# Remainders of the sparse attention's keys in one half of the partitions, and their logits pass over 64 rows

## The chip, the cores and the metric

The kernel runs on one core of one Trainium2 chip. The metric is the device time of one execution in microseconds (us): the median of three runs of the kernel before is 1380.08 us (1379.23 to 1384.18). A core has a matrix engine (PE, with its weight loads shown as PEld), a vector engine (DVE), an engine for activations (ACT), a general engine (POOL) and one that issues transfers (SP). They work through queues of their own and wait for each other by semaphores.

## The reference

One layer of a decoder trunk, 1024 tokens wide 1024, all in f32. A combined projection feeds three groups: a gated linear recurrence (4 heads, HGRN2), a sparse attention (4 heads of 64) and a cross-attention to 256 memory tokens. A projection back and a gated feed-forward follow. The change concerns the sparse attention alone:

```python
def dsa_mix(q, k, v, iq, ik, iw, q_gain, k_gain):
    ...
    q = rmsnorm(q, q_gain).astype(f32)
    k = rmsnorm(k, k_gain).astype(f32)
    ...
        score = jnp.where(visible[None], score, -jnp.inf)
        _, idx = lax.top_k(score, topk)
        ...
        logits = jnp.einsum('bqhd,bqkhd->bhqk', qb, kg) * (SA_DH ** -0.5)
        logits = jnp.where(valid[:, None], logits, -jnp.inf)
        p = jax.nn.softmax(logits, axis=-1)
        return jnp.einsum('bhqk,bqkhd->bqhd', p, vg)
```

The kernel does not gather keys: it computes the logits of all keys up to the end of the query's block and adds a mask of the kept ones.

## The kernel before, in words

**Precision.** The matmuls of f32 operands run in fp32r. For them an operand is written as a head (`hi`, an ACT copy into fp32r) and a remainder (`lo`, the operand minus its head), and a product is built from hi x hi, hi x lo and lo x hi.

**Operands of the sparse attention.** A head has 64 dimensions, half of the 128 partitions. Heads come in pairs: pair m holds head h = 2m + j in the partitions `ROWS[j]`, 0 to 63 or 64 to 127. For queries, `stack` (lines 245 to 255) writes the head of the query into `ROWS[j]` of a tile `qst[h][hf]` and its remainder into the other half, so that one tile of 128 partitions holds both (`hf` is the half of the 1024 tokens). For keys, lines 807 to 819 fill two tiles per head and half: `kst[h][0]` has the key's head in both halves of the partitions (two ACT copies, L818), `kst[h][1]` the key's remainder in both halves (two subtractions, L819: DVE writes the head's own half, POOL the other one).

**Logits.** `sa_logits` runs over blocks of 128 queries from the last (b = 7) to the first, and over 4 heads. A block sees 128 (b + 1) keys, taken in chunks of up to 512 columns, each chunk with a PSUM bank of its own (tag `lg`). A chunk is two matmuls that add up (L838): the query tile is the stationary operand, 128 rows by 128 columns; the moving operand is `kst[h][0]` and then `kst[h][1]`. The first gives (hi + lo of q) x hi of k, the second (hi + lo of q) x lo of k. There are 48 chunks. DVE then adds the mask and takes the maximum (L840).

**Order.** The stages of an item (logits; exponential on ACT and scaling on POOL, L849 and L855; transposes on PE, L864; the product with the values, L883, whose output is 64 partitions wide) run as a pipeline of four, and between its steps stand `fillers`: the last head of the recurrence (L518 to L612) and first parts of the output projection (L186). A scheduler that follows a model of the time sets the order on each engine. The names: `sap` is the preparation of the sparse attention, `sat` the attention, `hg` the recurrence, `wo` the output projection; `sap_h` are the tiles of `qst` and `kst`.

L271, which is named later, transposes eight rows of indexer weights with eight matmuls of 8 rows at partition 64; L117 and L118 split an operand into head and remainder; L144 to L151 are the small steps of an inverse root on DVE.

Of the kernel before, what the change touches and what calls it, by code (L numbers as in the profile page):

```python
# [9 lines left out]
F32 = mybir.dt.float32  # L10
# [5 lines left out]
AF = mybir.ActivationFunctionType  # L16
# [26 lines left out]
def hybrid_block(ctx, tc, xT, memT, wch, wikw, wv, wkm, wvm, woa, wob, wfi, wfo,  # L43
                 vec, cst, lvl, out):
    nc = tc.nc
    V, S, G, T = nc.vector, nc.scalar, nc.gpsimd, nc.tensor
# [13 lines left out]
    def nm(p):  # L60
        cnt[0] += 1
        return f"{ph[0]}_{p}{cnt[0]}"
# [4 lines left out]
    def bank(tag):  # L67

        return pp.tile([128, 512], F32, tag=tag, name=nm(tag))

    def xt(i, shape, dt=F32):
        return xp.tile(shape, dt, tag=f"x{i}", name=nm(f"x{i}_"))
# [4 lines left out]
    def ht(p, k, hf):  # L77
        return hp.tile([128, 512], F32R, tag=f"h{p}{k}{hf}", name=nm("h"))

    def hs(hf):  # L80
        return slice(hf * 512, hf * 512 + 512)

    def bs(b):
        return slice(b * 128, b * 128 + 128)
# [160 lines left out]
    def stack(st, ps, hf, rs, gain=None):  # L245

        o = slice(64 - rs.start, 128 - rs.start)
        if gain is None:
            S.activation(st[rs, hf], ps[rs], AF.Copy)
            V.tensor_sub(st[o, hf], ps[rs], st[rs, hf].bitcast(F32))  # L250
        else:
            g = vs[rs, gain:gain + 1]
            S.activation(st[rs, hf], ps[rs], AF.Copy, scale=g)
            V.scalar_tensor_tensor(st[o, hf], ps[rs], g, st[rs, hf].bitcast(F32),
                                   op0=ALU.mult, op1=ALU.subtract)

    ROWS = (slice(0, 64), slice(64, 128))
# [53 lines left out]
    for k in range(8):  # L311
        src = mT[k // 4][:, k % 4, :]
# [13 lines left out]
    for m in range(2):  # L326
# [15 lines left out]
        r = bank("sm")[:, :256]  # L342
        token_rows(r, rk, 2)
        V.scalar_tensor_tensor(kr, kr, vs[:, V_MK:V_MK + 1], r, op0=ALU.mult, op1=ALU.mult)
        for j in range(2):
            rs = slice(64 * j, 64 * j + 64)
# [4 lines left out]
    for g in range(2):  # L351
        w = load_page(wvm[g], 4, 256)
        for tt in range(2):
            i = 0
            for pw, p in PASSES:
                for k in range(4):
                    T.matmul(acc[tt][:, :256], mn[p][g][:, k, bs(tt)], w(pw, k),
                             start=g == 0 and i == 0, stop=g == 1 and i == 11)
# [10 lines left out]
    for t2 in range(4):  # L369
# [3 lines left out]
        for b in range(2, 8):  # L373
            for j in range(2):
                h = 2 * t2 + j
                for c0 in range(0, 128 * (b + 1), 512):
                    c1 = min(128 * (b + 1), c0 + 512)
                    lg = bank(("lg", "rc")[j])
                    for p in range(2):
                        T.matmul(lg[:, :c1 - c0], iqs[t2 % 2][j][:, b // 4, bs(b % 4)], ik[p][:, c0:c1],  # L380
                                 start=p == 0, stop=p == 1)
# [25 lines left out]
    def q_scale():  # L407

        wide = lambda t: t.unsqueeze(2).to_broadcast([128, 8, 2])
        for m in range(2):  # L410
            V.tensor_mul(qrs[:, m], qsq[:, m], wide(rn2))
        flat = qrs.rearrange("p a b c -> p (a b c)")
        narrow_rstd(flat, flat, 64, 32)
        for m in range(2):
            V.scalar_tensor_tensor(qrs[:, m], qrs[:, m], 0.125, wide(rn), op0=ALU.mult,
                                   op1=ALU.mult)
# [379 lines left out]
    qst = [[None, None] for _ in range(4)]  # L796
# [9 lines left out]
    kst = [[[None, None], [None, None]] for _ in range(4)]  # L806
    for hf in range(2):
        for m in range(2):
            for j in range(2):
                h = 2 * m + j  # L810
                if m == 0:
                    qst[h][hf] = ht(0, h, hf)
                    stack(qst[h][hf].unsqueeze(1), sqr[0][:, hs(hf)], 0, ROWS[j], V_SAQ)
                for p in range(2):
                    kst[h][p][hf] = ht(1 - p, h + 4 * p, hf)
                src = kr[m][ROWS[j], hs(hf)]
                for o, e in ((ROWS[j], V), (ROWS[1 - j], G)):
                    S.activation(kst[h][0][hf][o], src, AF.Copy)  # L818
                    e.tensor_sub(kst[h][1][hf][o], src, kst[h][0][hf][ROWS[j]].bitcast(F32))  # L819
    q_scale()  # L820

    ph[0] = "sat"
# [3 lines left out]
    def sa_logits(t):  # L826
        b, h = t["b"], t["h"]
        nk = 128 * (b + 1)
        m, j = h // 2, h % 2
        i = t["i"]  # L830
        mask = sc[b] if b >= 2 else tri[:, 128 * (1 - b):256]
        P = t["P"] = xt((0, 1, 12)[i % 3], [128, 1024])
        mx = t["mx"] = np_.tile([128, 3], F32, tag="mz", name=nm("mz"), bufs=5)
        for c in range(0, (nk + 511) // 512):
            c0, c1 = 512 * c, min(nk, 512 * c + 512)
            lg = bank("lg")
            for p in range(2):
                T.matmul(lg[:, :c1 - c0], qst[h][b // 4][:, bs(b % 4)],  # L838
                         kst[h][p][c][:, :c1 - c0], start=p == 0, stop=p == 1)
            V.tensor_tensor_reduce(P[:, c0:c1], lg[:, :c1 - c0], mask[:, c0:c1], 1.0,  # L840
                                   -3.0e38, ALU.add, ALU.max, mx[:, c:c + 1])
        rq = t["rq"] = qrs[:, m, b, j:j + 1]
        if nk > 512:
            V.tensor_max(mx[:, 0:1], mx[:, 0:1], mx[:, 1:2])
        V.scalar_tensor_tensor(mx[:, 0:1], mx[:, 0:1], -1.0, rq, op0=ALU.mult, op1=ALU.mult)
# [51 lines left out]
    def sparse_attention():  # L897
        items = [dict(b=b, h=h, i=4 * n + h) for n, b in enumerate(range(7, -1, -1))
                 for h in range(4)]
        return pipeline(items, (sa_logits, lambda t: (sa_exp(t), sa_scale(t)), sa_turn, sa_out))  # L900
# [275 lines left out]
    for n, j in enumerate([2 * i for i in range(NP)] + [2 * i + 1 for i in range(NP)]):  # L1176
        if n < 12:
            wo_[j] = halves(xt(PAGES[n], [128, 1024]))
        else:
            i, hf = divmod(n - 12, 2)  # L1180
# [88 lines left out]
    def four(slot, m, hf):  # L1269

        t = []

        def add(store):
            def begin():
                if not t:
                    t.extend(again(slot, m, hf) + again(slot + 1, m + 2, hf))
                return done

            def done(i, ps):
                V.tensor_add(t[i], t[i], ps)  # L1280
                if store:
                    nc.sync.dma_start(out[bs(m + i), hs(hf)], t[i])
            return begin
        return add
# [3 lines left out]
    c = four(0, 0, 0)  # L1288
# [85 lines left out]
```

## Time and profile before

| | |
|---|---|
| median of 3 runs | 1380.08 us (1379.23 to 1384.18) |
| the profiled execution | 1380.01 us |
| its span, first to last instruction | 1378.2 us, mean granted clock of TensorE 0.973 |
| PE busy | 1299.7 us (94%), 8072 matmul records |
| DVE busy | 1051.9 us (76%) |
| ACT busy | 691.2 us (50%) |
| POOL busy | 476.4 us (35%) |
| the chain that ended last | PE 68%, DVE 20%, ACT 7% of the span |

The busy shares are averages over a long program. The preparation of the sparse attention, the attention and the feed-forward behind it have different limits, so the view of a stretch tells more than these shares. The end of a matmul's record is modelled; the distance from one start to the next tells what it costs.

### The profile page before, as it was taken

To read this page: it belongs to the slowest core of one execution; us is meant where nothing else is said; L and a number is where in the kernel's file an instruction comes from. 1 tells how busy PE (TensorE), PEld (TensorE's weight loads), DVE (VectorE), ACT (ScalarE), POOL (GpSimd) and SP (SyncE) were. 2 spreads that over 40 slices of the span, in tenths; PEclk is the share of its full clock that TensorE was granted. 3 is DMA by queue.
4 is the path that set the end of the run, shared out by engine and by line. 5 is a ranking of instruction groups with operands and counts; after the bars stand their busy time and mean duration, and the time that the engine had idled before them with its cause. 6 is when DMAs were issued, how large, how long until landed. Compare 5 with 4: busy or idle time off the path is not lost.

```text
span 1378.2 us, 21967 instructions
## 1 busy us (share of the span) xinstructions
PE 1299.7 (94%) x8072; PEld 1067.1 (77%) x8072; DVE 1051.9 (76%) x2027; ACT 691.2 (50%) x1369; POOL 476.4 (35%) x395
## 2 busy tenths in 40 slices
PE   7989999989999995999997999999999998999998
PEld 4767797769887874876886888888888887878887
DVE  8696998895486789775679778777787766696764
ACT  7555879968823252756454333333333334334442
POOL 2311134364375642424005233332332210484520
PEclk9999999979999996899999999999999999999999
DMA  6110010000101101013331332222222219754241
GB/s 238 64 45 16 17 50 29 32 32 33 46 17 47 36 17 47 2 62 129 122 109 62 115 115 100 99 86 106 100 103 104 92 55 352 242 192 144 84 146 62
DMA packets 53245, 122.19 MB, mean 89 GB/s; under 512 B 6033, under 2 KB 6161, under 8 KB 53137
## 3 DMA queue, kind: packets, MB, share of 16 engines
q1 hardware_dynamic: 52848, 120.58, 25.2%
q8 instruction: 63, 1.03, 0.3%
q14 instruction: 46, 0.37, 0.1%
q10 hardware_dynamic: 288, 0.22, 0.1%
HBM read 92.19 MB, written 28.57 MB: 88 GB/s over the span
## 4 chain that ended last, share of the span: by engine, by line
PE 68%; DVE 20%; ACT 7%; issue 3%; DMA 1%; POOL 1%; DVEq 0%; SPq 0%; ACTq 0%; POOLq 0%
PE ff_lg L1103 17%; PE ff_rc L1103 12%; PE hg_mm L186 4%; PE fo_mm L1266 4%; PE fo_sm L1266 4%; DVE idx_x L646 4%; PE wo_mm L1062 3%; PE fo_rc L1266 3%; PE fo_lg L1266 3%; PE wo_sm L1062 2%; PE sap_mm L186 2%; PE idx_mm L186 2%; ACT idx_x L643 1%; DVE idx_x L388 1%; PE sat_sm L864 1%
## 5 line engine op out<-in xcount | busy, mean ns | idle before, releaser
L117 ACT ACTIVATE ff_whi<-ff_x 128x512 fp32r<-128x512 f32 x112 | 70.0, 629 | 125.3 <-PE ff_rc L1103 69.1
L643 ACT ACTIVATE idx_x<-idx_x,packs 128x896 int8<-128x896 f32 (+3 forms) x128 | 105.6, 825 | 29.8 <-DVE packs L662 22.2
L1103 PE MATMUL ff_lg<-wo_h,ff_whi 128*128 128x512 f32 x396 | 104.2, 389 | 0.0
L186 PE MATMUL hg_mm<-xn_h,hg_whi 128*128 128x512 f32 x384 | 97.3, 399 | 0.0
L1103 PE MATMUL ff_rc<-wo_h,ff_whi 128*128 128x512 f32 x308 | 90.8, 395 | 0.0
L1103 PE MATMUL ff_lg<-wo_x,ff_whi 128*128 128x512 f32 x308 | 83.8, 400 | 5.6 <-ACT ff_tmp L1110 4.8
L118 DVE TENSOR_TENSOR ff_wlo<-ff_x,ff_whi 128x512 fp32r<-128x512 f32 x112 | 82.6, 745 | 7.1 <-ACT ff_whi L117 4.0
L1103 PEld LDWEIGHTS ff_lg<-wo_h,ff_whi 128*128 128x128 f32 x396 | 74.5, 188 | 15.4
L186 PEld LDWEIGHTS hg_mm<-xn_h,hg_whi 128*128 128x128 f32 x384 | 71.6, 191 | 15.0 <-issue 0.9
L118 POOL TENSOR_TENSOR hg_wlo<-hg_wst,hg_whi 128x512 fp32r<-128x512 f32 x32 | 42.9, 1357 | 112.6 <-ACT hg_whi L117 81.7
L1103 PEld LDWEIGHTS ff_lg<-wo_x,ff_whi 128*128 128x128 f32 x308 | 56.8, 189 | 24.2 <-ACT ff_whi L117 7.7
L646 DVE TENSOR_SCALAR_CACHE_REDUCE idx_x<-idx_x,packs 128x1024 int8<-128x1024 f32 x64 | 68.8, 1075 | 1.0
L1103 PEld LDWEIGHTS ff_rc<-wo_h,ff_whi 128*128 128x128 f32 x308 | 58.8, 191 | 12.4
L1103 PE MATMUL ff_rc<-wo_x,ff_whi 128*128 128x512 f32 x220 | 64.4, 390 | 0.1
L528 POOL TENSOR_TENSOR hg_x<-hg_x,hg_x 128x256 f32<-128x256 f32 x56 | 48.1, 876 | 34.5 <-PE hg_rc L518 23.4
L1103 PE MATMUL ff_lg<-wo_h,ff_wlo 128*128 128x512 f32 x198 | 55.6, 389 | 0.0
L388 DVE SCALAR_TENSOR_TENSOR idx_x<-idx_tmp,packs,idx_x 128x512 f32<-128x512 f32 (+2 forms) x70 | 46.1, 709 | 12.3 <-ACT idx_tmp L383 11.9
L118 DVE TENSOR_TENSOR fo_wlo<-fo_tmp,fo_whi 128x512 fp32r<-128x512 f32 x33 | 32.9, 996 | 27.3 <-ACT fo_whi L117 27.3
L186 PE MATMUL hg_mm<-xn_h,hg_wlo 128*128 128x512 f32 x192 | 50.9, 397 | 0.0
L1103 PEld LDWEIGHTS ff_rc<-wo_x,ff_whi 128*128 128x128 f32 x220 | 41.2, 188 | 9.1 <-ACT ff_whi L117 0.6
L1103 PE MATMUL ff_rc<-wo_h,ff_wlo 128*128 128x512 f32 x154 | 45.6, 389 | 0.0
L1041 POOL TENSOR_TENSOR ff_x<-ff_wst,ff_wst 128x512 f32<-128x512 f32 x7 | 14.0, 2003 | 91.0 <-PE wo_sm L1062 74.7
(485 smaller groups left out, 3681.3 us busy)
## 6 DMA issues: line engine op xcount, KB each, us to landing
gd<-ff_m SPq DMA_DIRECT2D x77, 256.0 KB, 2.0
fo_x<-gd SPq DMA_DIRECT2D x77, 256.0 KB, 4.1
ff_x<-wfi SPq DMA_DIRECT2D x16, 512.0 KB, 3.3
ff_wst<-wfi SPq DMA_DIRECT2D x14, 512.0 KB, 3.2
ff_m<-wfi SPq DMA_DIRECT2D x14, 512.0 KB, 3.2
hg_wst<-wch SPq DMA_DIRECT2D x12, 512.0 KB, 3.3
fo_x<-wfo SPq DMA_DIRECT2D x24, 256.0 KB, 5.2
fo_h<-wfo SPq DMA_DIRECT2D x20, 256.0 KB, 4.4
```

The source lines that it names most:

```text
L117: S.activation(hi, src, AF.Copy)
L118: (eng or V).tensor_sub(lo, src, hi.bitcast(F32))
L186: T.matmul(ps[:M, :], w(pw, k), h[p][k][hf], start=i == 0, stop=i == len(order) - 1)
L388: V.scalar_tensor_tensor(sc[b][:, c0:c1], rl[:, :c1 - c0], iww[:, b, h:h + 1], sc[b][:, c0:c1], op0=ALU.mult, op1=ALU.add)
L528: G.tensor_mul(Kv[:, :, 0, :], Kv[:, :, 0, :], fr.to_broadcast([128, n, w]))
L643: S.activation(waste[S][:, :nk], sc[b], AF.Sign, bias=fl[:, j:j + 1], accum_out=ct[:, j:j + 1])
L646: eng.tensor_scalar(waste[eng][:, :nk], sc[b], fl[:, j:j + 1], None, op0=ALU.is_ge, op1=ALU.add, accum_out=ct[:, j:j + 1])
L864: T.transpose(tb[:, bs(kb - g0)], P[:, bs(kb)], ident)
L1041: G.tensor_sub(s3, a11, a21)
L1062: mm = T.matmul(ps, lhs, rhs, start=i == 0, stop=i == len(steps) - 1)
L1103: mm = T.matmul(ps, w[pw][:, bs(k)], HB[u][k][p], start=first and i == 0, stop=i == 11, skip_group_check=True)
L1266: T.matmul(banks[m], w[i][pw][:, bs(m)], b[i][p], start=first and i == 0 and n == 0, stop=i == NP - 1 and n == 2, skip_group_check=True)
```

## The change

POOL's subtraction is gone: the key's remainder is written only into the head's own half of the partitions, by DVE as before. ACT still copies the head into both halves. In the logits the first matmul of a chunk is as before; the second takes only the 64 rows `ROWS[j]` of both operands. There the query tile holds its head, so the second product is now hi of q x lo of k, and the product of the two remainders is left out.

```diff
--- before.py
+++ after.py
@@ -814,9 +814,10 @@
                 for p in range(2):
                     kst[h][p][hf] = ht(1 - p, h + 4 * p, hf)
                 src = kr[m][ROWS[j], hs(hf)]
-                for o, e in ((ROWS[j], V), (ROWS[1 - j], G)):
-                    S.activation(kst[h][0][hf][o], src, AF.Copy)
-                    e.tensor_sub(kst[h][1][hf][o], src, kst[h][0][hf][ROWS[j]].bitcast(F32))
+                o = ROWS[j]
+                for r in (o, ROWS[1 - j]):
+                    S.activation(kst[h][0][hf][r], src, AF.Copy)
+                V.tensor_sub(kst[h][1][hf][o], src, kst[h][0][hf][o].bitcast(F32))
     q_scale()
 
     ph[0] = "sat"
@@ -834,9 +835,9 @@
         for c in range(0, (nk + 511) // 512):
             c0, c1 = 512 * c, min(nk, 512 * c + 512)
             lg = bank("lg")
-            for p in range(2):
-                T.matmul(lg[:, :c1 - c0], qst[h][b // 4][:, bs(b % 4)],
-                         kst[h][p][c][:, :c1 - c0], start=p == 0, stop=p == 1)
+            for p, rs in ((0, slice(0, 128)), (1, ROWS[j])):
+                T.matmul(lg[:, :c1 - c0], qst[h][b // 4][rs, bs(b % 4)],
+                         kst[h][p][c][rs, :c1 - c0], start=p == 0, stop=p == 1)
             V.tensor_tensor_reduce(P[:, c0:c1], lg[:, :c1 - c0], mask[:, c0:c1], 1.0,
                                    -3.0e38, ALU.add, ALU.max, mx[:, c:c + 1])
         rq = t["rq"] = qrs[:, m, b, j:j + 1]
```

On POOL, between the recurrence's steps (L528) of its head 2 and those of its head 3, stand the eight subtractions of the keys:

```order
 L528 TENSOR_TENSOR hg_x_568_3372<-hg_x_568_3372,hg_x_569_3373 128x8x32 x2
 L528 TENSOR_TENSOR hg_x_568_3372<-hg_x_568_3372,hg_x_569_3373 128x4x64 x2
-L819 TENSOR_TENSOR sap_h_5513<-sap_m_667_4665,sap_h_5512 64x512
-L819 TENSOR_TENSOR sap_h_5522<-sap_m_667_4665,sap_h_5521 64x512
-L819 TENSOR_TENSOR sap_h_5528<-sap_m_668_4666,sap_h_5527 64x512
-L819 TENSOR_TENSOR sap_h_5534<-sap_m_668_4666,sap_h_5533 64x512
-L819 TENSOR_TENSOR sap_h_5543<-sap_m_667_4665,sap_h_5542 64x512
-L819 TENSOR_TENSOR sap_h_5552<-sap_m_667_4665,sap_h_5551 64x512
-L819 TENSOR_TENSOR sap_h_5558<-sap_m_668_4666,sap_h_5557 64x512
-L819 TENSOR_TENSOR sap_h_5564<-sap_m_668_4666,sap_h_5563 64x512
 L528 TENSOR_TENSOR hg_x_642_4459<-hg_x_642_4459,hg_x_643_4460 128x256 x2
 L528 TENSOR_TENSOR hg_x_642_4459<-hg_x_642_4459,hg_x_643_4460 128x128x2 x2
```

Nothing else moves on POOL; the rows around the gap follow each other directly. On PE no instruction is added, removed or moved. One place in the attention, before, between a product with the values (L883) and the recurrence (L594); `sap_h` are the key tile and the query tile of two chunks, of 512 and 256 keys:

```order
L883 MATMUL sat_mm_6114<-sat_x_814_6050,sap_x_552_3146 64x128
L838 MATMUL sat_lg_6163<-sap_h_5521,sap_h_5548 128x512
L838 MATMUL sat_lg_6163<-sap_h_5522,sap_h_5548 128x512
L838 MATMUL sat_lg_6167<-sap_h_5551,sap_h_5548 128x256
L838 MATMUL sat_lg_6167<-sap_h_5552,sap_h_5548 128x256
L594 MATMUL hg_rc_6251<-hg_x_602_3847,hg_x_666_4648 128x128
```

The same place with the change, where lines behind 819 have a number higher by one:

```order
L884 MATMUL sat_mm_6106<-sat_x_814_6042,sap_x_552_3146 64x128
L839 MATMUL sat_lg_6155<-sap_h_5520,sap_h_5543 128x512
L839 MATMUL sat_lg_6155<-sap_h_5521,sap_h_5543 128x512
L839 MATMUL sat_lg_6159<-sap_h_5546,sap_h_5543 128x256
L839 MATMUL sat_lg_6159<-sap_h_5547,sap_h_5543 128x256
L594 MATMUL hg_rc_6243<-hg_x_602_3847,hg_x_666_4648 128x128
```

The order is the same; the second and the fourth of the L839 rows now use 64 of the array's 128 rows.

## Rows read from the trace of the kernel before

**Rows 1.** Busy time by stretch: PE, PEld, DVE, ACT, POOL, clock, DMA.
```profile
502.00:534.00 32.00, 21.70 (x110) 18.62 (x108) 30.86 (x74) 19.78 (x33) 12.42 (x8) 0.79 0.15 50
...
553.90:634.00 80.10, 79.75 (x636) 64.59 (x636) 58.09 (x213) 51.91 (x115) 26.84 (x34) 0.97 0.08 28
```

**Rows 2.** Timeline, PE: start, us, operation, idle before.
```profile
522.02 2.05 PE L172 MATMUL sap_sm<-packs,sap_tmp 128*128 128x128 f32 x8 [8.58 <-DVE sap_tmp L169]
```

**Rows 3.** Timeline, DVE, from 502 to 518 us.
```profile
503.56 1.66 DVE L819 TENSOR_TENSOR sap_h<-sap_m,sap_h 64x512 fp32r<-64x512 f32 x1
...
510.53 0.68 DVE L819 TENSOR_TENSOR sap_h<-sap_m,sap_h 64x512 fp32r<-64x512 f32 x1
...
511.14 1.25 DVE L149 SCALAR_TENSOR_TENSOR sap_abx<-sap_abx 128x8 f32<-128x8 f32 x1
...
512.42 0.17 DVE L150 TENSOR_TENSOR sap_abx<-sap_abx 128x8 f32<-128x8 f32 x1
...
516.14 0.65 DVE L150 TENSOR_TENSOR sap_abx<-sap_abx 128x8 f32<-128x8 f32 x1
```

**Rows 4.** Timeline, POOL, from 495 to 535 us.
```profile
502.37 3.98 POOL L819 TENSOR_TENSOR sap_h<-sap_m,sap_h 64x512 fp32r<-64x512 f32 x2 [12.29 <-PE sap_mm L186]
...
510.57 6.19 POOL L819 TENSOR_TENSOR sap_h<-sap_m,sap_h 64x512 fp32r<-64x512 f32 x4 [4.23 <-ACT sap_h L818]
...
526.34 2.62 POOL L819 TENSOR_TENSOR sap_h<-sap_m,sap_h 64x512 fp32r<-64x512 f32 x2 [9.57 <-ACT sap_h L818]
```

**Rows 5.** Timeline, DVE, at 526 us.
```profile
526.49 1.15 DVE L151 SCALAR_TENSOR_TENSOR hg_abx<-hg_abx 128x8 f32<-128x8 f32 x1
```

**Rows 6.** Timeline, ACT, and one operation of DVE, 509 to 525 us.
```profile
509.86 2.58 ACT L818 ACTIVATE sap_h<-sap_m 64x512 fp32r<-64x512 f32 x4 [4.21 <-DVE sap_m L752]
...
515.56 0.52 ACT L117 ACTIVATE wo_whi<-wo_wst 128x384 fp32r<-128x384 f32 x1
...
518.80 0.54 DVE L118 TENSOR_TENSOR wo_wlo<-wo_wst,wo_whi 128x384 fp32r<-128x384 f32 x1
...
524.78 0.68 ACT L253 ACTIVATE sap_h<-sap_mm,packs 64x512 fp32r<-64x512 f32 x1 [3.61 <-DVE sap_h L254]
```

**Rows 7.** Matmuls of L838 by stretch: PE, PEld, clock, DMA.
```profile
534.00:553.90 19.90, 2.04 (x4) 1.16 (x4) 0.61 0.01 3
553.90:634.00 80.10, 20.10 (x80) 12.78 (x80) 0.97 0.08 28
```

**Rows 8.** Chain that ended last, 553 to 580 us: start, us, work.
```profile
559.71 0.81 PE sat_lg L838 x4
560.52 0.44 PE sat_sm L864 x4
...
562.21 0.59 PE sat_sm L864 x4
...
563.82 1.01 PE sat_lg L838 x4
```

**Rows 9.** Timeline, PE, around L271, and eight passes at 511 us.
```profile
51.89 0.84 PE L186 MATMUL idx_mm<-xn_h,xn_wlo 128*72 128x512 f32 x3
52.66 1.05 PE L271 MATMUL idx_sm<-packs,idx_tmp 8*128 8x8 f32 x8
53.65 0.45 PE L186 MATMUL idx_mm<-xn_h,xn_wlo 128*72 128x512 f32 x1
53.93 0.64 PE L332 MATMUL mkv_mm<-mkv_x,mkv_whi 128*128 128x256 f32 x4
...
511.46 1.98 PE L186 MATMUL sap_mm<-xn_h,sap_wlo 128*128 128x512 f32 x8
```

**Rows 10.** Chain that ended last, at 536 and at 596 us.
```profile
536.44 1.71 PE sat_lg L838 x4
...
596.45 0.68 DVE wo_m L920
...
600.88 0.90 PE sat_lg L838 x4
```

## The prediction

> **What bounds the kernel now.** I read the busy time by stretch first, then the chain of work that ended last, then the timeline of single engines where the diff acts. The change touches two stretches, and they have different limits.
>
> From 502 to 534 us the keys and queries of the sparse attention are split into head and remainder. There DVE is busy 30.86 of 32.00 us and PE only 21.70 [rows 1]; PE stands still for 8.58 us until DVE has written a tile (L169) at 522 [rows 2]. What DVE does is therefore the time of this stretch. From 553.9 to 634 us, the sparse attention itself, PE is busy 79.75 of 80.10 us [rows 1] and the chain runs from one PE piece to the next. So in the first stretch microseconds are won on DVE, in the second they are lost on PE, and the diff does one of each.
>
> **First part: eight subtractions leave POOL.** They are L819's second halves, 64x512 each; DVE keeps its eight, ACT its sixteen copies (L818). The trace shows no wait for one of POOL's remainders, so its 12.4 us of POOL time [rows 1] are worth nothing as such. What counts is what DVE does while POOL runs them. At 503.56 DVE's own L819 takes 1.66 us; the same operation at 510.53, begun just before POOL's next group, takes 0.68 [rows 3]. POOL was inside L819 from 502.37 to 506.35 and from 510.57 to 516.76 [rows 4]. Long DVE operations there go from 0.68 to 1.65 or so three times (503.56, and alike at 505.24 and 512.62), which is 0.98 + 0.97 + 0.99 = 2.94. Tiny ones of 0.17 (as at 512.42) become 1.25 and 0.65, and between these 1.11 at 514.32 [rows 3]: 1.08 + 0.94 + 0.48 = 2.50. A last one, at 526.49, takes 1.15 [rows 5] under POOL's last pair [rows 4]: 0.98. In all 6.4 us of DVE's time appear only while POOL subtracts, and I expect all of it to go.
>
> How much reaches PE? ACT could take over as the limit. Its run of splits starts at 509.86, behind L752 on DVE [rows 6], thus after the first two long stalls, and comes 1.95 us earlier; ACT itself gets no faster. DVE's L118 at 518.80 needs the ACT copy of 515.56, which ends at 516.08 [rows 6], afterwards at 516.08 - 1.95 = 514.13. DVE can therefore come to it at about 514.2, 4.6 us earlier, not 2.94 + 2.50 = 5.4. Of the last 0.98 I count 0.9, because the DVE operation behind it (L840) reads PE's first logits and may have to wait for them. Together 5.5 us, between 0 (if the long DVE operations have another reason) and 6.4.
>
> **Second part: 48 remainder passes over 64 rows.** Each block of up to 512 keys has two matmuls of L838. Their moving columns stay the same, and so does the time that they stream; half the rows idle. Both instructions remain. What is new is that the array goes from 128 rows to 64 and back. The order on PE is the same, so the switches can be counted in it. In the PE-bound stretch stand 80 matmuls of L838 [rows 7], 40 remainders. Each is one switch in. Behind 13 comes the next block's full pass, behind 12 a transpose (L864, one L571), behind 5 another full matmul (L186, L578, L594); that is one switch out each. Behind the other 10 comes a half-width matmul (L883 and its like), before which the array changes its shape already. New switches: 40 + 30 = 70.
>
> Their price: before shows switches between full and half width of the output. Two 512-column and two 384-column passes of L838 take 0.81 us on the chain behind a full-array matmul (559.71), and 1.01 behind half-width ones (563.82; 1.02 at 571.38). Four transposes take 0.44 without and 0.59 with a switch [rows 8]. So 0.20 before L838, 0.15 before a transpose. A switch of rows occurs in one place only, L271, whose matmuls have 8 rows. Eight undisturbed 512-column passes take 1.98 us and three 0.84, so each further one (1.98 - 0.84) / 5 = 0.228 [rows 9]. The three before L271 begin at 51.89 and L271 at 52.66: 0.77 - 3 x 0.228 = 0.09 more. On the way out L186 at 53.65 has 0.28 to the next start at 53.93, 0.05 more, besides what came before it [rows 9]. So rows do cost, at least 0.09 a switch. Which end holds? L271's matmuls have 8 columns and are paced by their weight loads anyway, so a load that can no longer hide under the matmul before would not show at its entry. A 512-column pass hides its load, and loses that cover. The remainder pass is much nearer to L838 behind a switch, and I take 0.20 (0.15 before transposes).
>
> Sum on PE: 40 x 0.20 + 13 x 0.20 + 12 x 0.15 + 5 x 0.20 = 8.0 + 2.6 + 1.8 + 1.0 = 13.4. Between 596.45 and 600.9 the chain is on DVE [rows 10]; four remainders and three switches out stand there (1.2 us) and are free, which leaves 12.2. Before 553.9 stand eight more remainders: six fall in the DVE-bound stretch and I count nothing; two (4 matmuls, in a stretch whose granted clock is 0.61 [rows 7]) are on the chain at 536.44, 1.71 us for what takes 0.81 to 1.02 later [rows 8, 10]: four switches, 0.7 us. PE loses 12.9.
>
> The Trainium skill speaks against such a change: in TensorEngine Tiling (Array Packing), section Key Properties, it says that changing the tiling mode drains TensorE. The rows agree that a switch costs, 0.09 at the least; the page gives no price, and with 0.09 for each switch the sum would be the second rival's.
> The same skill, TensorE: Matmul & The Clock Gate, section LDWEIGHTS, counts a weight load by its columns at 1.2 per ns, whatever the rows: 0.107 us for 128 columns. An estimate from it, 0.09 + 0.107, is again 0.20 and leaves the sum where it is.
>
> **Sum.** 12.9 - 5.5 = +7.4 us. The profiled execution took 1380.01 us (span 1378.2 and 1.8 around it), 0.07 below the median, so 1380.1 + 7.4 = 1387.5.
>
> **Rivals.**
> 1. Not slower: a 64-row pass switches nearly for free, because the tile of 64 rows lies inside the array just used and its load may go ahead. Then only DVE's gain is left: 1380.1 - 5.5 = 1374.6. For it: no row here has 64 rows. Against: L271, with 0.09 more. It decides if a switch costs under 5.5 / 65 = 0.085 us, 65 being 12.9 / 0.20. Chance 0.08.
> 2. Only the drain counts, 0.09 to 0.12: 65 x 0.10 = 6.5, less 5.5, +1: 1381. For it: the entry to L271. Against: 0.20 at L838. Chance 0.20.
> 3. DVE's gain does not arrive: ACT, which gets no faster, gives the 5.5 back. Then 1380.1 + 12.9 = 1393. For it: ACT works without a gap from 509.86 to 521. Against: it then stands idle for 3.61 us, waiting for DVE [rows 6]. Chance 0.10.
> 4. Gaps at the switches lower the granted clock between 554 and 634, where it is 0.97 now. L838's 80 matmuls take 20.1 us there [rows 7]; if a tenth of the 80 us ran at half clock, 8 us more: 1395. For it: 70 new gaps. Against: the clock is full there though half-width switches are already frequent. Chance 0.07.
>
> My forecast, 1384 to 1391 us, has the remaining 0.55.
>
> **How the numbers follow.** A change under 0.5%, 6.9 us, can hardly be told from none. The forecast's sum lies just above that: of its 0.55 I put 0.33 above 1387.0 and 0.22 below. Slower: 0.33 + 0.10 + 0.07 = 0.50. Same: 0.22 + 0.20 + 0.06 of the first rival = 0.48. Faster: 0.02, the first rival with all 6.4 us and an earlier rise of the clock. Both signs hold chance, so the range goes from rival 2's lower side, 1380, to rival 3's 1393; outside it stay rivals 1 and 4 and a little of 3. The forecast's own range is 1384 to 1391.
>
> **What would show each step.** No L819 on POOL; DVE's operations between 502 and 517 at 0.68 and 0.17 us, none above 1; PE's wait for L169 near 4 us instead of 8.58; the first PE piece of the attention (553.90 now) near 549. Then, on the chain, four passes of L838 that took 0.81 take about 1.4 (three switches inside), transposes behind a remainder 0.59 instead of 0.44, and PE gets to 634's place near 641. The prediction is wrong if L838 keeps its 0.81, if DVE stays slow without POOL, or if the granted clock of the second stretch falls.

## The result, and the profile after

The changed kernel takes 1389.86 us, the median of six runs (1387.09 to 1391.71), against 1379.84 for the kernel before in the same sitting: a ratio of 1.0067, 95% interval 1.0055 to 1.0079. The profiled execution took 1389.45 us with a span of 1387.7, that is 9.5 more than before. The sum had said +7.4 and 1387.5 us.

The busy time by stretch, for the kernel after, with the columns of [rows 1]; the granted clock of the middle one was 0.61 before [rows 7]:

```profile
502.00:534.00 32.00, 28.03 (x119) 20.57 (x118) 29.27 (x86) 19.62 (x32) 0.00 (x0) 0.72 0.15 49
534.00:553.90 19.90, 11.97 (x421) 9.29 (x422) 16.43 (x49) 5.27 (x10) 11.54 (x13) 0.50 0.02 4
553.90:634.00 80.10, 80.10 (x558) 57.81 (x553) 53.29 (x187) 43.10 (x90) 22.16 (x27) 0.98 0.08 27
```

POOL is empty in the first stretch. PE is busy for 28.03 us there instead of 21.70, with 119 matmuls instead of 110. In the last it has no gap at all and issues 558 matmuls in the time of 636.

DVE in the timeline of the kernel after (start, us, operation, idle before), to be read beside [rows 3]:

```profile
502.08 0.68 DVE L820 TENSOR_TENSOR sap_h<-sap_m,sap_h 64x512 fp32r<-64x512 f32 x1 [0.93 <-PE sap_mm L186]
...
503.40 0.69 DVE L820 TENSOR_TENSOR sap_h<-sap_m,sap_h 64x512 fp32r<-64x512 f32 x1
...
511.47 0.16 DVE L150 TENSOR_TENSOR sap_abx<-sap_abx 128x8 f32<-128x8 f32 x1
...
514.01 0.56 DVE L118 TENSOR_TENSOR wo_wlo<-wo_wst,wo_whi 128x384 fp32r<-128x384 f32 x1 [0.28 <-ACT wo_whi L117]
```

What took 1.66 takes 0.69, the small steps take 0.16, and at 514.01 DVE waits for ACT's copy, the limit that the prediction had put there at about 514.2. PE in the timeline of the kernel after:

```profile
517.25 2.05 PE L172 MATMUL sap_sm<-packs,sap_tmp 128*128 128x128 f32 x8 [3.97 <-DVE sap_tmp L169]
...
520.66 2.94 PE L839 MATMUL sat_lg<-sap_h,sap_h 128*128 128x512 f32 x4
...
525.26 5.84 PE L839 MATMUL sat_lg<-sap_h,sap_h 128*128 128x512 f32 x8
...
532.64 2.94 PE L839 MATMUL sat_lg<-sap_h,sap_h 128*128 128x512 f32 x4
...
551.74 1.97 PE L865 MATMUL sat_sm<-packs,sat_x 128*128 128x128 f32 x8 [0.81 <-POOL sat_x L856]
```

and the same passes in the timeline of the kernel before:

```profile
525.43 2.05 PE L838 MATMUL sat_lg<-sap_h,sap_h 128*128 128x512 f32 x4
...
528.84 3.44 PE L838 MATMUL sat_lg<-sap_h,sap_h 128*128 128x512 f32 x8
...
534.73 1.71 PE L612 MATMUL hg_rc<-packs,hg_x 128*128 128x128 f32 x8 [2.45 <-DVE hg_x L606]
...
536.11 2.04 PE L838 MATMUL sat_lg<-sap_h,sap_h 128*128 128x512 f32 x4
...
553.90 1.97 PE L864 MATMUL sat_sm<-packs,sat_x 128*128 128x128 f32 x8 [0.85 <-POOL sat_x L855]
```

The wait for L169 fell from 8.58 [rows 2] to 3.97, 4.6 us, as worked out. But the first eight chunks are now slow: 2.94 for 2.05, 5.84 for 3.44, 2.94 for 2.04. So the first transposes of the attention come only 2.16 us earlier, not 4.8. The chain that ended last, for the kernel after, says who holds them up:

```profile
517.25 2.05 PE sap_sm L172 x8
519.30 1.50 PE sap_sm L403 x8
520.80 2.80 PE sat_lg L839 x4
523.60 1.80 PE sap_sm L403 x8
525.40 5.70 PE sat_lg L839 x8
531.10 1.90 PE hg_rc L612 x8
532.99 2.60 PE sat_lg L839 x4
535.59 0.63 PE hg_rc L518 x32
...
557.58 1.40 PE sat_lg L839 x4
558.99 0.59 PE sat_sm L865 x4
...
562.43 1.60 PE sat_lg L839 x4
```

From 517.25 to 536.2 every piece is PE's. Before, this stretch was DVE's, but PE had little to spare in it: behind the first twelve passes it waited only 2.45 us for DVE (L606, the row at 534.73), and with the change it does not wait there at all. The last three rows answer to [rows 8]: four passes 1.40 for 0.81, which is 0.197 for each of three switches; transposes 0.59 for 0.44; behind a half-width product 1.60 for 1.01. These are the prices of the prediction.

The views of the logits' line count the idle time ahead of its instructions, matmuls and weight loads together; after and then before:

```profile
  issue: 12.8, 48
```

```profile
  issue: 1.5, 7
```

All of these waits stand on PEld, the queue of weight loads; asked for PE alone, the view has none. Of the 48 after, 32 stand ahead of a load of 64 rows and 16 ahead of one of 128, so loads wait at changes of shape in both directions. Loads (PEld) in the timeline of the kernel after, one from the stretch at half clock and two from full clock, and then four in the kernel before:

```profile
525.96 0.29 PEld L839 LDWEIGHTS sat_lg<-sap_h,sap_h 64*128 64x128 f32 x1 [0.44 <-issue]
...
557.74 0.18 PEld L839 LDWEIGHTS sat_lg<-sap_h,sap_h 64*128 64x128 f32 x1 [0.24 <-issue]
558.17 0.19 PEld L839 LDWEIGHTS sat_lg<-sap_h,sap_h 128*128 128x128 f32 x1 [0.25 <-issue]
```

```profile
559.44 0.76 PEld L838 LDWEIGHTS sat_lg<-sap_h,sap_h 128*128 128x128 f32 x4
```

Before, the load of the second of these passes starts at 559.55 and its matmul at 559.78, so the load lies under the matmul ahead of it. At a switch the load starts only with its own matmul, both at 557.74. The prices are close to the length of such a load: 0.197 beside 0.18 to 0.19, about 0.15 ahead of a transpose whose load takes 0.14, and at half clock 0.30 beside 0.29. So what a switch costs here looks like one weight load that is no longer hidden.

**Where the 9.5 us are.** First transposes: -2.16. From there to the issue of the output projection's weights at the end of the attention, which the chain shows at 635.22 before and at 644.00 after: 644.00 - 551.74 = 92.26 for 635.22 - 553.90 = 81.32, +10.94. Behind it +0.7, which I did not trace.

### The profile page after: what moved, and what is told of

Its sections match the earlier page's. It is cut to its first block, busy times and chain, and to the rows that moved or that the text cites. A ratio compares the mean times of both kernels' runs of the same rounds, so it can differ in the third digit from the quotient of the medians.

```text
span 1387.7 us, 21951 instructions
## 1 busy us (share of the span) xinstructions
PE 1316.7 (95%) x8072; PEld 1069.9 (77%) x8072; DVE 1045.2 (75%) x2027; ACT 691.2 (50%) x1369; POOL 463.1 (33%) x387
## 3 DMA queue, kind: packets, MB, share of 16 engines
HBM read 92.19 MB, written 28.57 MB: 87 GB/s over the span
## 4 chain that ended last, share of the span: by engine, by line
PE 69%; DVE 19%; ACT 7%; issue 3%; DMA 1%; POOL 1%; DVEq 0%; SPq 0%; ACTq 0%; POOLq 0%
PE ff_lg L1104 17%; PE ff_rc L1104 12%; PE hg_mm L186 4%; PE fo_mm L1267 4%; PE fo_sm L1267 4%; DVE idx_x L646 4%; PE wo_mm L1063 3%; PE fo_rc L1267 3%; PE fo_lg L1267 3%; PE sat_lg L839 3%; PE wo_sm L1063 2%; PE sap_mm L186 2%; PE idx_mm L186 2%; PE sat_sm L865 1%; DVE idx_x L388 1%
## 5 line engine op out<-in xcount | busy, mean ns | idle before, releaser
L528 POOL TENSOR_TENSOR hg_x<-hg_x,hg_x 128x256 f32<-128x256 f32 x56 | 48.2, 879 | 72.1 <-PE hg_rc L518 59.4
L1104 PEld LDWEIGHTS ff_rc<-wo_h,ff_whi 128*128 128x128 f32 x308 | 58.9, 191 | 12.4
L388 DVE SCALAR_TENSOR_TENSOR idx_x<-idx_tmp,packs,idx_x 128x512 f32<-128x512 f32 (+2 forms) x70 | 46.1, 710 | 10.6 <-ACT idx_tmp L383 10.3
L856 POOL TENSOR_SCALAR sat_x<-sat_x,sat_mz 128x1024 f32<-128x1024 f32 (+7 forms) x32 | 26.2, 819 | 64.6 <-DVE sat_mz L855 38.2
L118 DVE TENSOR_TENSOR fo_wlo<-fo_h,fo_whi 128x512 fp32r<-128x512 f32 x31 | 32.9, 1061 | 17.8 <-ACT fo_whi L117 17.8
```

Of the source, the lines that this page charges most:

```text
L118: (eng or V).tensor_sub(lo, src, hi.bitcast(F32))
L388: V.scalar_tensor_tensor(sc[b][:, c0:c1], rl[:, :c1 - c0], iww[:, b, h:h + 1], sc[b][:, c0:c1], op0=ALU.mult, op1=ALU.add)
L528: G.tensor_mul(Kv[:, :, 0, :], Kv[:, :, 0, :], fr.to_broadcast([128, n, w]))
L856: G.tensor_scalar(P[:, :nk], P[:, :nk], mx[:, 2:3], 1.0, op0=ALU.mult, op1=ALU.mult)
L1104: mm = T.matmul(ps, w[pw][:, bs(k)], HB[u][k][p], start=first and i == 0, stop=i == 11, skip_group_check=True)
```

## The experiments

Theory: 0.20 us a switch (0.15 before a transpose), less what DVE gains. Rival for the part that the sum got wrong: the early passes cost more than a switch, because they run at half clock and PE has become the limit. Ratios are to the kernel before in the same sitting. One point of time serves for all traces below: the end of the last eight passes of `sap_mm`, in before 511.46 + 1.98 = 513.44 [rows 9]; the expectations count from a point 0.4 us earlier.

**1. First part alone.** The other half of the remainder tile is filled with zeros by POOL, and both passes keep 128 rows, so that no switch is added and the logits have the value of the change. The diff is against the changed kernel, as the others are where no other kernel is named.

```diff
                 V.tensor_sub(kst[h][1][hf][o], src, kst[h][0][hf][o].bitcast(F32))
+                G.memset(kst[h][1][hf][ROWS[1 - j]].bitcast(F32), 0.0)
...
-            for p, rs in ((0, slice(0, 128)), (1, ROWS[j])):
-                T.matmul(lg[:, :c1 - c0], qst[h][b // 4][rs, bs(b % 4)],
-                         kst[h][p][c][rs, :c1 - c0], start=p == 0, stop=p == 1)
+            for p in range(2):
+                T.matmul(lg[:, :c1 - c0], qst[h][b // 4][:, bs(b % 4)],
+                         kst[h][p][c][:, :c1 - c0], start=p == 0, stop=p == 1)
```

> The first part of the change alone: POOL's eight subtractions are replaced by eight memsets of zero into the same halves, and the remainder pass keeps its 128 rows. The result is the changed kernel's, the order on PE, DVE and ACT that of before. Theory (two separate effects: DVE is freed of POOL's subtractions, PE pays for switches): no switch is added and DVE loses its 6.4 us of long operations, so 5.5 us under before, 1374.5. Rival 1 (any POOL work in this stretch holds DVE up, a memset too): as before, 1380. Rival 2 (the long DVE operations have another reason): as before, with DVE at 1.66 us while POOL is idle.

Measured: 1376.93 us (1372.1 to 1377.99), ratio 0.9963 [0.9947, 0.9979], span 1375.1; DVE's gain arrives. Two rows of POOL and two of DVE from this kernel's timelines:

```profile
504.53 2.25 POOL L821 MEMSET sap_h<- 64x512 f32 x4 [12.19 <-PE sap_mm L186]
...
515.10 2.24 POOL L821 MEMSET sap_h<- 64x512 f32 x4 [8.31 <-PE sap_mm L186]
```

```profile
505.84 0.69 DVE L820 TENSOR_TENSOR sap_h<-sap_m,sap_h 64x512 fp32r<-64x512 f32 x1
...
515.42 0.68 DVE L820 TENSOR_TENSOR sap_h<-sap_m,sap_h 64x512 fp32r<-64x512 f32 x1
```

DVE's subtraction runs in the middle of POOL's writes and takes 0.68 to 0.69. So it was not POOL's being busy that slowed DVE, but POOL's subtractions. The Trainium skill, SBUF — State Buffer, section Who interferes with whom, says that a DVE instruction with two inputs in SBUF contends with a GpSimd instruction that reads SBUF and not with one that only writes it. The rows agree: 1.66 beside a subtraction [rows 3, 4], 0.68 beside a write. Counted from the common point, the first transposes come 40.46 - 35.29 = 5.2 us earlier, where the sum had 5.5.

**2. Second part alone.** POOL's subtractions stay; the second pass takes 64 rows. Against the kernel before:

```diff
-            for p in range(2):
+            for p, rs in ((0, slice(0, 128)), (1, ROWS[j])):
```

> The second part alone: POOL still subtracts, the remainder pass uses 64 rows. Order of all engines as before. Theory: the eight remainder passes before 535 us lie behind a late DVE and cost little, the 40 others cost what the changed kernel showed, 10 to 12 us, so 1390 to 1393. Rival (the switches cost less, and something else slowed the changed kernel, as a lower granted clock): 1380 to 1385. If the two parts simply add up, this run and the run with zeros together are as far from before as the changed kernel is, +9.5 us.

Measured: 1394.32 us, ratio 1.0100 [1.0085, 1.0116], somewhat over the range expected. In the timeline of this kernel DVE is slow again, and PE's wait for L169 is the 8.58 us of before:

```profile
503.44 1.65 DVE L819 TENSOR_TENSOR sap_h<-sap_m,sap_h 64x512 fp32r<-64x512 f32 x1
```

```profile
521.90 2.05 PE L172 MATMUL sap_sm<-packs,sap_tmp 128*128 128x128 f32 x8 [8.58 <-DVE sap_tmp L169]
...
529.91 5.84 PE L838 MATMUL sat_lg<-sap_h,sap_h 128*128 128x512 f32 x8
...
556.24 1.97 PE L864 MATMUL sat_sm<-packs,sat_x 128*128 128x128 f32 x8 [0.85 <-POOL sat_x L855]
```

The early passes are as slow as in the change, and the first transposes come 42.92 us after the common point, 42.92 - 40.46 = 2.5 later than before. So the eight early passes are not covered even where DVE is as late as it was: the passes and the L403 between them got 3.5 us longer by L612, and PE had 2.45 to spare there.

Experiments 1 and 2 together: -0.37% and +1.00% make +0.63%, the change +0.67%: the parts add up.

**3. The order of an item's passes written as two full ones, then two remainders.** If a switch has a price, fewer of them cost less.

```diff
-        for c in range(0, (nk + 511) // 512):
...
+        for p, rs in ((0, slice(0, 128)), (1, ROWS[j])):
+            for c, c0, c1, lg in chunks:
```

> The changed kernel with the passes of an item grouped: full pass of both chunks, then remainder pass of both chunks, instead of full, remainder, full, remainder. The same 48 passes of 64 rows, but 16 items have one switch in and one out in place of two each. Theory (the price is per switch, 0.20 us, 0.3 at half clock): 32 switches fewer, 6.4 us and about 1 more in the first items, less a little because the first chunk's maximum starts a pass later: 1383 to 1385. Rival (a pass over 64 rows is slow in itself, whatever stands beside it): 1389 to 1391, as the changed kernel.

Measured: 1386.95 us, ratio 1.0047 [1.0033, 1.0060]; a miss. The scheduler kept the written order in only 5 of the 16 items with two chunks, so that the program has 10 switches fewer than the change (225 against 235), and not the 17 fewer that all 16 groups give (experiment 5). It stands 0.20% or 2.8 us under the change, with ±0.18% on the difference: the sign and the size fit ten prices, but can't measure one.

**4. Both passes over 64 rows.**

```diff
-            for p, rs in ((0, slice(0, 128)), (1, ROWS[j])):
+            for p, rs in ((0, ROWS[j]), (1, ROWS[j])):
```

> The changed kernel with both passes over the 64 rows of the head's own half: it leaves out the product of the query's remainder with the key's head. 96 passes of 64 rows, and within an item no switch at all. Theory (price per switch): one switch in and at most one out per item, as in the grouped kernel: 1383 to 1386. Rival (64-row passes are slow in themselves, 0.2 to 0.4 us each): 48 more slow passes, 1398 to 1408.

Measured: 1383.18 us, ratio 1.0015 [1.0007, 1.0024]. Two pieces of the chain that ended last in this kernel, each four passes of 64 rows behind a half-width matmul:

```profile
557.70 1.02 PE sat_lg L839 x4
...
560.69 1.01 PE sat_lg L839 x4
```

They are as long as four passes of 128 rows in that place, 1.01 [rows 8]. So a pass of 64 rows behind another one is neither faster nor slower, and the price is in the change of shape. The time as a whole says less, since its order differs too.

**5. The grouped order held.** Each remainder pass is tied behind the full ones.

```diff
+        for ch in chunks:
+            last = logits(0, slice(0, 128), *ch)
+        for ch in chunks:
+            with tc.issue_after(last.ins):
+                last = logits(1, ROWS[j], *ch)
```

> The changed kernel with the passes of an item grouped and the grouping held against the scheduler (each remainder pass is issued behind the last full pass of its item): full, full, remainder, remainder in all 16 items of two chunks. The same 48 passes of 64 rows, 68 more switches than before instead of 85; the order around the items changes too. Theory (price per switch, 0.20 us): 17 fewer, 3.4 us under the changed kernel, 1385 to 1387. Rival (a 64-row pass is slow in itself): 1389 to 1391.

Measured: 1381.71 us, ratio 0.9989 [0.9975, 1.0004]. Four passes with one switch inside take, on the chain of this kernel, one price more than 1.01:

```profile
552.07 1.20 PE sat_lg L839 x4
...
555.57 1.21 PE sat_lg L839 x4
```

The time is under the ranges of both the theory and the rival. 17 switches fewer than the change (218 against 235) are worth 3.4 us, but the kernel is 0.78% or some 10 us under it. Its first transposes came 28.28 us after the common point, after the change 38.46. Two rows of DVE in this kernel's timeline, the first and the last step of the queries' inverse root:

```profile
527.75 0.17 DVE L144 TENSOR_SCALAR sap_abx<-packs 128x32 f32<-128x32 f32 x1
...
535.41 0.54 DVE L151 SCALAR_TENSOR_TENSOR packs<-sap_abx 128x32 f32<-128x32 f32 x1
```

That is 8.2 us from start to end. The kernel after has the same two rows so:

```profile
528.93 0.17 DVE L144 TENSOR_SCALAR sap_abx<-packs 128x32 f32<-128x32 f32 x1
...
547.21 0.59 DVE L151 SCALAR_TENSOR_TENSOR packs<-sap_abx 128x32 f32<-128x32 f32 x1
```

18.87 us, for its 15 steps lie between those of the recurrence's scan (L527 to L529 of before), which wait for PE and POOL. What holds the root holds the attention's first transposes. Experiments 8 to 10 follow this up.

**6 and 7. The 64 rows for some blocks of queries alone**: in 6 for b < 7, the forty later remainders; in 7 for b = 7, the first eight. Zeros and 128 rows elsewhere.

```diff
-            for p, rs in ((0, slice(0, 128)), (1, ROWS[j])):
+            for p, rs in ((0, slice(0, 128)), (1, ROWS[j] if b == 7 else slice(0, 128))):
```

> The kernel with zeros, with 64-row remainder passes only in the items of the blocks behind the first (b below 7): 40 passes, 70 more switches, all of them in the stretch that PE bounds at full clock. The order on every engine is that of the kernel with zeros, which was 5 us under before. Theory (0.20 us a switch, 0.15 before a transpose): 10 to 12 us over the kernel with zeros, 1387 to 1389. Rival (most of the loss lies in the first eight passes, at half clock): 1380 to 1384.

> The kernel with zeros, with 64-row remainder passes only in the four items of the first block (b = 7): 8 passes, 15 more switches, all before 540 us. Theory as the prediction had it (six of the eight lie behind a late DVE and are free): 0.7 us over the kernel with zeros, 1377 to 1378. Rival, from the trace of the changed kernel (freed of the long operations, DVE waits for PE there, whose passes at half clock cost 0.3 us more per switch): 3 us over the kernel with zeros, 1379 to 1381, and the granted clock stays at its lower level until the transposes.

Measured: 6 takes 1385.57 us, ratio 1.0026 [1.0012, 1.0040]; 7 takes 1379.08, ratio 0.9978 [0.9967, 0.9989]. Over the first part alone these are +0.63% (8.7 us, ±2.9) and +0.15% (2.1 us, ±2.7), so the times alone can't tell what the early passes cost. The traces can: with the early passes the first transposes come 37.21 - 35.29 = 1.9 us later, not 0.7, and with the late ones the first matmul of the output projection behind the attention comes 131.02 - 120.28 = 10.7 us later, within the 10 to 12 expected. At that matmul the two make 10.7 + 1.7 = 12.4, where the change stands 135.09 - 120.28 = 14.8 over the first part alone (the table under experiments 9 and 10 has these places). What the rival said of the clock did not come: in kernel 7 the granted clock is 0.50 from 516.5 to 533.6, 1.00 to 540.4 and 0.50 to 554.1, not one block as in the change, and the last four of the early passes take 1.99 us there and not 2.94.

**8. Held order without switches**: kernel 5's code with 128 rows for both passes, and the zeros. Against kernel 5, without the line for the zeros:

```diff
-                last = logits(1, ROWS[j], *ch)
+                last = logits(1, slice(0, 128), *ch)
```

> The first part of the change alone (zeros, written by POOL, in the other half of the key's remainder tile; both passes of a chunk over 128 rows), with the passes of an item held in the grouped order: both first passes, then both second ones. There is no 64-row pass, so no switch that before does not have. The grouped and held kernel stood 10.8 us under the changed kernel, of which 17 switches fewer explain 3.4 (17 x 0.20); 7.4 are left. Theory: these come from the order in which the scheduler puts the recurrence's steps and the passes when the passes are held, and not from 64 rows; its first transposes began 28.66 us after the end of the preparation, where the changed kernel took 38.85. Then this kernel goes under the first part alone (0.9963 of before) by 4 to 7 us, to 1370 to 1374, and its first transposes begin within about 30 us; its order is not the same as the grouped and held kernel's, as the scheduler puts other fillers, so not all of the 7.4 need come. Rival: the order gained only because it let switches fall behind other work; without switches there is nothing to gain, and it stays within 0.2% of the first part alone, at 1375 to 1379. Against each other the prices of a chunk's switches also show: four passes behind a full-array matmul should take 0.81 again, whatever their order.

Measured: 1377.56 us, ratio 0.9975 [0.9965, 0.9985]; the rival's number. But the scheduler laid the root between the scan's steps again (15.94 us, first transposes at 35.36), so the early root was not there to be judged.

**9 and 10. The root in one piece.** DVE's products of the scan wait until the root's last step is issued; 9 with the zeros and 128 rows, 10 with the change (the diff is against kernel 1 and against the change). Their orders on PE, DVE and ACT are the same, with 169 and 247 changes of shape.

```diff
+    def held_back():
+        return tc.issue_after(roots[0]) if roots else nullcontext()
...
-            V.tensor_mul(Qv[:, :, 1, :], Qv[:, :, 1, :], fl.to_broadcast([128, n, w]))
+            with held_back():
+                V.tensor_mul(Qv[:, :, 1, :], Qv[:, :, 1, :], fl.to_broadcast([128, n, w]))
...
-    q_scale()
+    roots.append(q_scale())
```

> The first part of the change alone (zeros in the other half of the key's remainder tile, both passes over 128 rows), and the queries' inverse root in one piece: DVE's products of the recurrence's scan (L527 of before) of the last head are held until the root's last step (L415) has been issued. Nothing is left out. Only the order changes: in the grouped and held kernel the root took 8.2 us, from L144 to the write of packs, and its first transposes came 28.66 us after the end of the preparation; in the first part alone it took 16.3 us, its 15 steps lying between those of the scan, and the first transposes came after 35.68. Theory: the root's place is the reason for what the grouped and held kernel had over its 17 switches, 7.4 us. Then the root takes about 8 us here, the first transposes come 6 to 8 us earlier, part of it is given back where the chain goes through DVE, and as the new order has 19 more changes of shape (169 against 150, 0.2 us each = 3.8) the time is 1370 to 1375. Rival: what the attention gains there waits later for the scan that was held, and the time stays at the first part's 1375 to 1379, or above.

> The changed kernel with the same hold on the scan. All engines have the order of the kernel with the first part alone and the hold, without POOL's eight writes; 247 changes of shape stand against 169. Theory: 78 more switches at 0.2 us, a few of them at 0.3 and a few behind other work: 13 to 16 us over that kernel, and thus 1384 to 1390, at or under the changed kernel. Rival: with the root early PE runs without gaps sooner, its clock rises sooner, and the early switches cost no more than at full clock: 10 to 12 us over it.

Measured: 9 takes 1374.86 us, ratio 0.9955 [0.9939, 0.9970]; 10 takes 1386.78, ratio 1.0032 [1.0018, 1.0047]. Worked out from the timelines of PE and DVE, in us; the last two columns are starts, counted from the common point:

| kernel | root, start to end | first transposes | first matmul of the output projection behind the attention |
|---|---|---|---|
| before | 15.87 | 40.46 | 126.37 |
| after | 18.87 | 38.46 | 135.09 |
| 1, zeros | 16.29 | 35.29 | 120.28 |
| 2, 64 rows, POOL subtracts | 18.34 | 42.92 | 139.24 |
| 5, grouped and held | 8.20 | 28.28 | 125.35 |
| 6, late rows | 15.99 | 34.97 | 131.02 |
| 7, early rows | 17.38 | 37.21 | 121.95 |
| 9, zeros, root first | 9.20 | 28.57 | 120.93 |
| 10, change, root first | 11.05 | 31.27 | 131.62 |

From 1 to 9 the early root gains 6.7 us at the first transposes, and all of it is gone at the end of the attention. The chain that ended last in kernel 9 shows where: where PE leaves its pieces, DVE and ACT take over.

```profile
541.56 1.98 PE sat_sm L873 x8
...
543.56 0.69 DVE sat_x L878
...
546.80 1.34 ACT sat_x L858 x2
...
556.76 1.23 ACT sat_x L858 x2
...
582.29 0.68 DVE sat_x L849
...
588.56 0.68 DVE hg_abx L151
```

1374.86 lies at the upper end of the theory's range, but 9 and 1 can't be told apart (their intervals overlap), so no gain is shown for the kernel without switches. With them, from the change to 10, 0.35% or 4.8 us remain, although 10 has 12 changes of shape more. From 10 to 5 there are 29 fewer, and 0.43% or 5.9 us: 0.20 each. Each of these differences carries about ±0.2%. Together they are the 0.78% of experiment 5, so that its surplus can be the root's place and the switches of the new order; that is argued from ratios and not shown piece by piece. From 9 to 10 there are 78 more, and 0.77% or 10.6 us (±2.9): 0.14 each, below the price and in the rival's 10 to 12. In kernel 10 the granted clock did rise sooner, from 536.6, but the first twelve early passes still take 2.94 and 5.84 us, so the rival's reason covers the last four at most. Why these switches cost less is not shown; a chain that leaves PE more often would do it.

Both kernels 1 and 9 beat the kernel before and the changed one; the zeros alone are the simplest version here that does.

## Why the prediction was right

Slower by 0.67%, forecast +0.54% with a range that holds the result. The mechanism was right in its two halves; one term of the sum was 2.6 us too small, one 1.3 too large, and 0.7 lie behind the attention, where I had nothing: 7.4 + 2.6 - 1.3 + 0.7 = 9.4. That the first two errors cancel in part is luck.

- **DVE's long operations come from POOL's subtractions: right.** All of these are gone; experiment 1 shows that POOL's reading subtraction did it, and 2 that they stay if it stays.
- **5.5 us of it reach PE: right.** 4.6 at L172 by ACT's limit, as worked out, and 5.2 at the first transposes when no switch is added (experiment 1). The third rival, that ACT gives it all back, is out.
- **0.20 us a switch, 0.15 before a transpose: right** at full clock: (1.40 - 0.81) / 3, 0.59 against 0.44, and 1.20 for one switch inside four passes. The first rival (nearly free) is refuted by these rows and by experiments 1 and 2; the second (0.10) by the same rows. The 0.09 at L271 [rows 9] was a lower bound, as argued. The prediction's remark that a pass "hides its load, and loses that cover" is what the loads of the kernel after show. Its estimate from the length of a load came to 0.20 by chance: a load of L838 takes 0.19 us in the trace, and not the shorter time that the estimate took.
- **12.2 us in the PE-bound stretch: 10.94 measured.** Most of the 1.3 can be found. Between 596.45 and 600.9 the trace has four switches out, not three, so that the free part is 1.55 us at these prices and not 1.2. And the last two remainders stand at 633.75 and 633.97, where the chain before has left PE, so that another 0.6 us is not paid:

```profile
633.86 0.62 ACT wo_h L117
```

- **0.7 us before 553.9: the step that failed.** The prediction says of the eight early remainders that "six fall in the DVE-bound stretch and I count nothing". But DVE's lead was no cover of that size. Before, PE had 2.45 us to spare behind these passes, 1.81 when DVE gains (kernel 1, the row at 531.41), and at half clock a switch costs more: (2.94 - 2.05) / 3 = 0.30, and eight passes in a row take 5.84, where kernel 1 takes 3.76 for them at the same granted clock of 0.50.

```profile
525.84 3.76 PE L840 MATMUL sat_lg<-sap_h,sap_h 128*128 128x512 f32 x8
531.41 1.97 PE L612 MATMUL hg_rc<-packs,hg_x 128*128 128x128 f32 x8 [1.81 <-DVE hg_x L606]
```

  Of DVE's 5.5 us, 2.16 were left at the first transposes, so the term measured 3.3 us and not 0.7 (3.2 against kernel 1: 38.46 - 35.29). DVE's gain is only a small part of the reason: in experiment 2, without it, the same passes cost 2.5. Experiment 7, with another course of the clock, puts it at 1.9.
- **The clock between 554 and 634: unchanged**, 0.98 for 0.97; the fourth rival is out. Earlier there is a difference that I had not forecast (below).

The Trainium skill's rule in TensorEngine Tiling (Array Packing), section Key Properties, that a change of the tiling mode drains TensorE, agrees with the rows: at a switch the next weight load starts only with its own matmul (557.74), and not under the one before it. By these runs a change of the rows costs as a change of the width does. A drain by itself, apart from the load, shows in no run here.

## What to carry to other kernels

Half the rows of a pass buy nothing in its time, and each change between 128 and 64 rows costs some 0.20 us at full clock, about the length of the weight load that it uncovers: where an operand lacks rows, write zeros into them once, with an instruction that reads nothing, and keep the shape. An added cost counts as hidden only against the wait that stands behind it on the same engine, and not because another engine bounds the stretch: here PE waited 2.45 us behind the early passes, and they grew by 3.5. Two operations, DVE with two inputs and POOL with a subtraction, should not run beside each other where DVE is the limit.

## What was not expected of the hardware

A switch costs about 0.30 us at a granted clock of 0.50, where it costs 0.20 at full clock: half as much again, and not twice. In the kernel after, the granted clock is 0.50 (1.2 GHz) in one block from 515.9 to 556.9 us, 41 us; in the kernel before it rose to 0.99 between 531.7 and 535.1, with the last of the eight passes that ran without a switch from 528.84 to 532.28, and to 1.00 between 538.5 and 541.9. With switches between the passes the first rise did not come; in kernel 2, with the same switches there, the clock stayed at 0.50 from 522 to 557 as well, but in kernel 7, which has them too, it rose from 533.6 to 540.4. So the switches alone don't decide it, and what the clock adds to the early term stays open. An earlier start of the attention by 7 us was worth nothing in a kernel that then waited for DVE and ACT (9 against 1).
